# Attention probabilities turned by VectorE and DRAM instead of by TensorE

## The chip, the cores and the metric

The kernel runs on one core of one Trainium2 chip. Its engines each work through an instruction queue of their own and wait for one another by semaphores: TensorE (PE in the profile; PEld is its weight load), VectorE (DVE), ScalarE (ACT), GpSimd (POOL) and SyncE (SP), whose queue issues most of the DMAs. The metric is the device time of one execution in microseconds, as a median of several runs. Lower is better.

## The reference

The program is two layers of a diffusion backbone over 512 latent tokens and 256 context tokens of width 1024, in fp32. Layer 0 has differential attention (8 heads, each with two score maps of head size 64), layer 1 grouped-query attention (8 query heads and 2 key/value heads of size 128). Context queries read only context keys, and the last layer computes no context output.

```
h = rms_norm(x, pre_g) * (1 + scale) + shift          # same for the context with its own scale, shift
q, k, v, z = split(h @ w_in)                          # q, k get rotary positions on latent tokens
p  = softmax(q k^T * scale)                           # per head, 512 x 768 for latent queries
layer 0: o = softmax1 @ v - lam * softmax2 @ v;  o = rms_norm(o, subln_g) * (1 - lam_init)
layer 1: o = softmax @ v
y  = (o * silu(z)) @ w_out
x  = x + gate * rms_norm(y, post_g)
```

`scale`, `shift` and `gate` come from `silu(c) @ ada_w + ada_b` (adaLN).

## The kernel before

Every fp32 product is taken as three passes: an operand is split into a rounded high part (`hi`, written by ScalarE) and the rest (`lo`, a subtraction on VectorE or GpSimd), and TensorE adds hi*hi, hi*lo and lo*hi (`mm3`). Weights come in tiles of 128x1024 (`raw`, two buffers) through SP's DMA queue; ScalarE writes `whi`, GpSimd or VectorE writes `wlo`, into one of three slots from which TensorE reads them.

Tokens are in 6 tiles of 128: 4 latent ones and 2 of context. A head's queries are worked in halves of 256 tokens ("a pair" below: two units of 128 queries). In layer 0 each head has two latent pairs (`ch` 0 and 1) and one of context (`ch` 2); in layer 1 two. For a pair the steps are:

- `s_units` (layer 0) or `s1_units` (layer 1): scores of 128 queries against 768 keys into the PSUM tiles `sc`, VectorE takes the row maximum, ScalarE the exponential with its sum, VectorE the reciprocal, GpSimd multiplies the row by it (`scaled`). In layer 0 the second map is multiplied by -lambda and added to the first on VectorE (`SCALAR_TENSOR_TENSOR p<-p,sm,p`). The result is `p`, 128 queries by 768 keys.
- `tstep` in `pv_steps` and `pv1_steps`: the next product needs keys on partitions, so TensorE transposes `p` block by block, four 128x128 blocks (two key tiles of two units) into one PSUM bank, by `nc.tensor.transpose(...)` with the identity `ident`; in the profile these are `bk<-ident,p`. ScalarE then writes `ah` and VectorE `al`, the split of that bank. Three tsteps make up a pair.
- `mstep` (`pv_mm`): `v` times `ah` and `al`, six matmuls of 256 columns for each tstep, accumulated over the three.

The `v` projection (`v_mm` in layer 0, `proj_tok` in layer 1) is turned round against the others: the tokens `h` are the stationary operand, 128 of them to a weight load, and the weights stream 256 columns. The profile writes such a matmul as `bk<-whi,h` (moving operand first).

The order of each engine is written by a planner. `flow` lays steps out by due times, with the projections' matmuls filled in between (`piece`), and `Plan.schedule` then sorts all operations by the prices of `Plan.price`, taking on each engine the operation that can start first. The result is fixed at build time: each engine, and SP's queue, then works in that order and waits where it must. All operations are recorded by one helper, so they all carry its line (L395 before); the profile is read by tile names.

Of the kernel before, what the change touches and what calls it, by code (L numbers as in the profile page):

```python
# [8 lines left out]
F32 = mybir.dt.float32  # L9
# [6 lines left out]
P = 128  # L16
# [31 lines left out]
WBUFS = 3  # L48
XE = [2, 2, 2, 2, 3, 3]
# [24 lines left out]
AB = 3  # L74
MEM = 227168
AHEAD_OPS = 1500
MARGIN = 1.08
SLOT = {}
# [28 lines left out]
class Plan:  # L107


    def __init__(self, mem, psum, sizes):  # L110
        self.mem, self.sizes = mem, sizes
        self.psum = dict(psum)
        self.banks = {t.tensor.name: t.free_size() for t in psum.values()}
        self.width = mem.shape[1]
        self.ops, self.offs, self.tail, self.seen = [], [0], None, {}
        self.marks = []
        self.pools, self.stack = [], {"left": [], "right": []}
        for q in QUEUE:
            setattr(self, q, Queue(self.add, QUEUE[q]))


    def pool(self, name, side="left", psum=False):
        return Pool(self, name, side, psum)

# [41 lines left out]
    def add(self, q, meth, args, kw):  # L166
# [14 lines left out]
        for aps_, w in ((ins, 0), (outs, 1)):  # L181
            for ap in aps_:
                if ap.space == bass.MemoryType.DRAM:
                    continue
                name, spans, parts = self.places(ap)
                if name not in self.banks:
# [103 lines left out]
    def schedule(self, rank):  # L290
# [15 lines left out]
        while len(order) < count:  # L306
# [27 lines left out]
            elif op.kind == "D":  # L334
                s = max(s, land.pop(0))
                go = s + (330 if e == "SP" else 450)
                dma = max(dma, go + 300) + op.cost / 350.0
                end = max(go + 1700 + op.cost / 350.0, dma) + (800 if op.cost == 131072 else 300)
# [47 lines left out]
class Emit:  # L386
# [7 lines left out]
    def add(self, eng, meth, args, kw):  # L394
        self.ops.append(getattr(eng, meth)(*args, **kw))  # L395
        return self.ops[-1]

# [81 lines left out]
def tile_backbone(  # L479
# [30 lines left out]
    ps1 = ctx.enter_context(pl.pool("ps1", psum=True))  # L510

# [24 lines left out]

    def mm3(o, ahi, alo, bhi, blo, start, stop):
# [4 lines left out]
    def pv_mm(o, vh, vl, c, ah, al, kt, first, last):  # L542
        terms = [(v, a, e) for v, a in ((vh, ah), (vl, ah), (vh, al)) for e in range(2)]
        for i, (v, a, e) in enumerate(terms):
            nc.tensor.matmul(o, v[:, kt + e, c], a[:, e * 256:e * 256 + 256], start=first and i == 0, stop=last and i == 5)
# [492 lines left out]
    def v_mm(o, w, t, k_lo=0, k_hi=KT, first=True, last=True):  # L1038
        for kt in range(k_lo, k_hi):
            sl = slice(t * P, (t + 1) * P)  # L1040
# [82 lines left out]
    with pl.pool("t0") as t0:  # L1123
# [140 lines left out]
        def s_units(h, qts):  # L1264
            res = []

            def unit(qt):
# [11 lines left out]
                prev = None  # L1279
                for j in range(nk // w):  # L1280
                    c = slice(k0 + j * w, k0 + j * w + w)
                    for i, (a, b) in enumerate(((qh, kh_), (qh, kl_), (ql, kh_))):
                        for m in (1, 0):
                            r = slice(m * 64, m * 64 + 64)
                            with after(prev), chained(prev):
                                prev = nc.tensor.matmul(
                                    sc[m][:, j if nk == T else m, :w], a[r, tok], b[r, c], start=i == 0, stop=i == 2)
                for m in range(2):
# [3 lines left out]
                    pt = t0.tile([P, T], F32, tag=f"p{m}", name=nm("p"), bufs=6 if m == 0 else 2)[:, :nk]  # L1292
                    pv_ = pt.rearrange("p (j n) -> p j n", j=2) if nk == T else pt
                    nc.scalar.activation(pv_, scv, AF.Exp, bias=mx, accum_out=l[:, m:m + 1])
# [5 lines left out]
                    else:  # L1300
                        nc.vector.tensor_tensor(r, r, nlam, ALU.mult)
                        nc.vector.scalar_tensor_tensor(ps_[0], pt, r, ps_[0], ALU.mult, ALU.add)
                        res.append(ps_[0])

            def unit_ctx():
# [3 lines left out]
                for qt in (NQ, NQ + 1):  # L1309
                    tok = slice(qt * P, (qt + 1) * P)  # L1310
                    for i, (a, b) in enumerate(((qh, kh_), (qh, kl_), (ql, kh_))):
                        for m in (1, 0):
                            r = slice(m * 64, m * 64 + 64)
                            with after(prev), chained(prev):
                                prev = nc.tensor.matmul(
                                    sc[m][:, qt - NQ, :C], a[r, tok], b[r, S:T], start=i == 0, stop=i == 2)
                l = [small(2), small(2)]
                pts = []
                for m in range(2):
                    mx = small(2)  # L1320
                    nc.vector.tensor_reduce(mx, sc[m][:, :, :C], AX.X, ALU.max, negate=True)
                    pt = t0.tile([P, T], F32, tag=f"p{m}", name=nm("p"), bufs=6 if m == 0 else 2)
# [19 lines left out]
        def pv_steps(h, at, ch, after, ts, ms):  # L1342
            kts = range(6) if ch < 2 else range(4, 6)
            st = {}

            def tstep(kt):
# [9 lines left out]
                nc.scalar.copy(ah, tr)  # L1356
                nc.vector.tensor_tensor(al, tr, f32(ah), ALU.subtract)
                st[kt] = ah, al

            def mstep(kt):  # L1360
# [6 lines left out]
                pv_mm(o, vh, vl, vc, ah, al, kt, kt == kts[0], kt == kts[-2])  # L1367
                if kt == kts[-2]:
# [5 lines left out]
                    nc.scalar.copy(gT[h][:, sl], o)  # L1374
# [185 lines left out]
    def proj_tok(o, w, t):  # L1560
# [132 lines left out]
    with pl.pool("t1", "right") as t1p:  # L1693
# [45 lines left out]
        def k_tr(m, kr):  # L1739
# [4 lines left out]
            sl = slice(m * P, (m + 1) * P)  # L1744
            nc.scalar.copy(kh[:, :, sl], tv)
            nc.vector.tensor_tensor(kl[:, :, sl], tv, f32(kh[:, :, sl]), ALU.subtract)
# [15 lines left out]
        for what, m in KV:  # L1762
# [7 lines left out]
            else:  # L1770
# [3 lines left out]
                run(proj_tok(o, wk if what == "k" else wv, m))  # L1774
# [74 lines left out]
        def s1_units(h, ms):  # L1849
            res = []  # L1850

            def unit(m):
# [4 lines left out]
                for j in range(2):  # L1857
                    c = slice(j * 384, j * 384 + 384)
                    mm3(sc[:, j, :384], qa[:, sl], qb[:, sl], kh[:, g, c], kl[:, g, c], True, True)
# [6 lines left out]
                pt = t1q.tile([P, T], F32, tag="p", name=nm("p"), bufs=5)  # L1866
                l = small()
                nc.scalar.activation(pt.rearrange("p (j n) -> p j n", j=2), scv, AF.Exp, scale=sr, bias=nmx, accum_out=l)
                nc.vector.reciprocal(l, l)
                scaled(EN1, pt, pt, l)  # L1870
                res.append(pt)
# [3 lines left out]
        def pv1_steps(h, at, ch, after, ts, ms):  # L1875
            g = h // 4
            st = {}

            def tstep(kt):
                tr = trp()  # L1880
                for e in range(2):
                    for i, a in enumerate(at):
                        nc.tensor.transpose(tr[:, e * 256 + i * P:e * 256 + (i + 1) * P], a[:, (kt + e) * P:(kt + e + 1) * P], ident)
# [4 lines left out]
                nc.scalar.copy(ah, tr)  # L1888
                nc.vector.tensor_tensor(al, tr, f32(ah), ALU.subtract)
                st[kt] = ah, al  # L1890

            def mstep(kt):
# [5 lines left out]
                pv_mm(o, vh, vl, c, ah, al, kt, kt == 0, kt == 4)  # L1898
                if kt == 4:
                    if ch == 0:  # L1900
                        gT1[h] = t1p.tile([P, 512], F32, tag="g1", name=nm("g1"), bufs=8)
                    (nc.scalar.copy if EG1 == "a" else nc.vector.tensor_copy)(gT1[h][:, ch * 256:ch * 256 + 256], o)
# [217 lines left out]
```

## Time and profile before

| | |
|---|---|
| Median of 3 runs | 808.6 us (806.29 to 809.25) |
| Profiled execution | 808.79 us, span 807.0 us |
| Granted TensorE clock | 0.993 |
| Busy, share of the span | PE 97%, weight loads 87%, DVE 59%, ACT 60%, POOL 54% |
| Instructions | 14,385 |
| DMA | 77.78 MB, mean 96 GB/s |

A row of the groups reads: line, engine, operation, out<-in with buffer numbers left out, partitions x elements, count, then busy time in us and the mean ns of one, then the idle time of the engine ahead of these instructions and what ended it. The busy time of a group on PE counts overlapped time once, so the mean of one matmul (from its start to its modelled end) is longer than the distance between two of them; how far apart they start is read from the timeline.

### The profile page before, as it was taken

Reading aid. Unit: us, or ns where it says so; the run is one execution under the profiler, and the core shown is the slowest. Engines: PE = TensorE matmul, PEld = TensorE weight load, DVE = VectorE, ACT = ScalarE, POOL = GpSimd, SP = SyncE. Lnnn points to the kernel's source line nnn. Section 1 sums busy time; section 2 is a strip of 40 time slices with the busy share of each in tenths; the row PEclk is TensorE's granted clock in tenths of the full one; section 3 lists DMA queues with packets and bytes.
Section 4 is the critical chain, followed back from the end, with each engine's and each line's share of the span. In section 5 each row is a group of like instructions: output and inputs, shape, how many; then the busy total and the mean of one; then the engine's idle time right before and its main releaser. Section 6 shows DMA issues by size and latency. Waiting matters only on the chain.

```text
span 807.0 us, 14385 instructions
## 1 busy us (share of the span) xinstructions
PE 786.4 (97%) x5482; PEld 699.8 (87%) x5482; DVE 473.6 (59%) x824; ACT 482.0 (60%) x1083; POOL 437.4 (54%) x512
## 2 busy tenths in 40 slices
PE   7899999999999999999999999999999999999997
PEld 5779888889887898797989998898999899898886
DVE  3425787774847546656546743788346455655625
ACT  5524577684565645666538843784466676768622
POOL 4545776874585654757923312366887646644101
PEclk9899999999999999999999999999999999999999
DMA  9951120132142431323430152035321200201112
GB/s 302 363 180 67 65 75 31 40 108 89 40 158 79 144 105 53 105 80 96 165 106 27 62 227 79 1 89 175 120 70 53 96 11 27 79 27 55 51 53 105
DMA packets 41541, 77.78 MB, mean 96 GB/s; under 512 B 3584, under 2 KB 18688, under 8 KB 41472
## 3 DMA queue, kind: packets, MB, share of 16 engines
q1 hardware_dynamic: 38048, 71.71, 27.4%
q10 hardware_dynamic: 3424, 5.15, 1.8%
q8 instruction: 43, 0.70, 0.4%
q14 instruction: 26, 0.21, 0.1%
HBM read 70.56 MB, written 2.10 MB: 90 GB/s over the span
## 4 chain that ended last, share of the span: by engine, by line
PE 91%; DVE 3%; ACT 2%; DMA 2%; issue 1%; SPq 0%; POOL 0%; ACTq 0%; DVEq 0%; POOLq 0%
PE bk L395 75%; PE sc L395 16%; DMA ag<-in_ada_w 1%; DMA raw<-in_post_g 1%; DVE gacc L395 1%; DMA gw<-in_ada_w 0%; ACT whi L395 0%; SPq L395 0%; DVE h L395 0%; ACT sq L395 0%; DVE hf L395 0%; ACT p L395 0%; DVE sw L395 0%; DVE gate L395 0%; ACT jk L395 0%
## 5 line engine op out<-in xcount | busy, mean ns | idle before, releaser
L395 PE MATMUL bk<-whi,h 128*128 128x256 f32 (+1 forms) x1184 | 244.6, 299 | 2.0 <-DVE kn L395 1.3
L395 PE MATMUL bk<-h,whi 128*128 128x512 f32 (+2 forms) x832 | 225.6, 351 | 0.0
L395 POOL TENSOR_TENSOR wlo<-raw,whi 128x256 fp32r<-128x256 f32 x200 | 162.5, 839 | 76.7 <-ACT whi L395 75.3
L395 PEld LDWEIGHTS bk<-whi,h 128*128 128x128 f32 x1184 | 191.0, 189 | 14.6 <-issue 4.9
L395 PE MATMUL bk<-wlo,h 128*128 128x256 f32 (+1 forms) x592 | 176.5, 299 | 0.0
L395 PEld LDWEIGHTS bk<-h,whi 128*128 128x128 f32 x832 | 144.1, 188 | 16.5 <-issue 4.4
L395 PE MATMUL bk<-h,wlo 128*128 128x512 f32 (+2 forms) x416 | 145.7, 351 | 0.0
L395 DVE TENSOR_REDUCE sm<-sc 128x1 f32<-128x768 f32 (+2 forms) x114 | 101.0, 897 | 25.7 <-PE sc L395 25.4
L395 PEld LDWEIGHTS bk<-wlo,h 128*128 128x128 f32 x592 | 111.7, 189 | 4.8 <-issue 1.4
L395 POOL TENSOR_SCALAR p<-p,sm 128x768 f32<-128x768 f32 (+1 forms) x80 | 68.4, 858 | 77.6 <-DVE sm L395 72.8
L395 DVE TENSOR_TENSOR al<-bk,ah 128x512 fp32r<-128x512 f32 x104 | 69.4, 685 | 39.3 <-ACT ah L395 38.8
L395 ACT CAST whi<-raw 128x1024 fp32r<-128x1024 f32 (+1 forms) x70 | 71.7, 1026 | 31.9 <-PE bk L395 27.7
L395 ACT ACTIVATE p<-sc,sm 128x768 f32<-128x768 f32 (+1 forms) x96 | 72.9, 762 | 21.6 <-DVE sm L395 15.6
L395 ACT CAST ah<-bk 128x512 fp32r<-128x512 f32 x104 | 59.0, 590 | 43.5 <-PE bk L395 43.1
L395 PEld LDWEIGHTS bk<-h,wlo 128*128 128x128 f32 x416 | 78.4, 188 | 7.5 <-issue 1.3
L395 PE MATMUL bk<-ident,p 128*128 128x128 f32 x416 | 64.3, 275 | 1.6 <-DVE ql L395 1.1
L395 PEld LDWEIGHTS bk<-ident,p 128*128 128x128 f32 x416 | 49.0, 141 | 11.4 <-issue 2.0
L395 DVE SCALAR_TENSOR_TENSOR p<-p,sm,p 128x768 f32<-128x768 f32 (+1 forms) x48 | 53.4, 1120 | 3.3 <-POOL p L395 0.5
L395 ACT ACTIVATE jk<-bk 128x128 f32<-128x128 f32 (+4 forms) x66 | 22.7, 345 | 53.5 <-PE bk L395 34.4
L395 POOL TENSOR_TENSOR sz<-sz,za 128x384 f32<-128x384 f32 (+1 forms) x24 | 29.4, 1227 | 40.3 <-ACT za L395 39.7
L395 PE MATMUL sc<-qk,qk 64*128 64x384 f32 (+1 forms) x480 | 50.6, 341 | 0.0
L395 DVE RECIPROCAL sm<-sm 128x1 f32<-128x1 f32 (+1 forms) x114 | 18.1, 159 | 52.0 <-ACT p L395 51.5
(191 smaller groups left out, 1375.5 us busy)
## 6 DMA issues: line engine op xcount, KB each, us to landing
raw<-in_a_w SPq DMA_DIRECT2D x30, 512.0 KB, 3.5
araw<-in_ada_w SPq DMA_DIRECT2D x12, 1024.0 KB, 5.3
raw<-in_b_w SPq DMA_DIRECT2D x20, 512.0 KB, 3.5
ag<-in_ada_w SPq DMA_DIRECT2D x32, 256.0 KB, 6.5
raw<-in_w_out SPq DMA_DIRECT2D x16, 512.0 KB, 3.6
sw<-qr ACTq DMA_DIRECT2D x32, 128.0 KB, 2.1
gw<-in_ada_w SPq DMA_DIRECT2D x8, 512.0 KB, 4.1
xt<-in_x SPq DMA_DIRECT2D x4, 512.0 KB, 5.1
```

Of the source, the lines that this page charges most:

```text
L395: self.ops.append(getattr(eng, meth)(*args, **kw))
```

## The change

For latent pairs TensorE's transposes are left out. The two units of a pair write one tile `pp` (128 queries by 24 key blocks by 2 units by 32), and `turn` does the rest: VectorE transposes every 32x32 block of it in place (one instruction over 1536 elements, `STREAM_TRANSPOSE`), SP stores the whole tile to a DRAM scratch `dr` (768 KB) and loads it back in four DMAs (192 KB each), each to one group of 32 partitions of the tile `at`, which then has keys on its partitions. `ah` and `al` are split from `at` in SBUF, no longer from a PSUM bank. The context pairs of layer 0 still go through TensorE.

Key j of block order no longer sits where it sat: partition 32a+j of key tile k holds latent token 4(32a+j)+k, or context token 2(32a+j)+k. So the `v` projection takes its 128 tokens with a step (`keys`: every fourth latent token, every second context token), and `k` is written in another order (`ordered`, in layer 0 three ACT casts and three POOL subtractions a head where two and two stood; in layer 1 in `k_tr`). The outputs of `pv_mm` come out as (block, unit, 32) and are put back by the copy into `gT` (`heads_out`). Buffers: `p` had 6 (layer 0) and 5 (layer 1), `pp` and `at` have 2 each, `ah` and `al` 2 where they had 3, `dr` 6. The planner prices a DMA of 192 KB at 570 ns of its queue and others at 450, and lets every landing be 1 us later.

```diff
+DPAD = 1000
-AB = 3
+AB = 2
+P0B = 2
+ATB = 2
+PPB = 2
+DRSPLIT = 1
+DRB = 6
+PEWAY = ((), ())
...
+    def keys(src, t):
+        if t < NQ:
+            return src[:, :S].rearrange("p (x k) -> p k x", k=4)[:, t]
+        return src[:, S:].rearrange("p (x k) -> p k x", k=2)[:, t - NQ]
+
+    def ordered(t, r, lo, k):
+        a = by_a(t, 192)[:, :, :P] if k == 4 else by_a(t, 192)[:, :, P:]
+        return a.rearrange("p a (k j) -> p a k j", k=k), r.rearrange("p (a j k) -> p a k j", a=4, k=k)
...
+            if moved:
+                d, b = by_a(o, 64), a.rearrange("p (b e x) -> p e b x", b=4, e=2)[:, e]
+            else:
+                d, b = o, a[:, e * 256:e * 256 + 256]
+            nc.tensor.matmul(d, v[:, kt + e, c], b, start=first and i == 0, stop=last and i == 5)
+
+    def turn(pool, pp):
+        flat = pp.rearrange("p b u x -> p (b u x)")
+        nc.vector.transpose(flat, flat)
+        at = pool.tile([P, 4, 384], F32, tag="at", name=nm("at"), bufs=ATB)
+        for lo in range(0, 4, 4 // DRSPLIT):
+            n = 4 // DRSPLIT
+            dr = drp.tile([P // DRSPLIT, 4 * 384], F32, tag="dr", name=nm("dr"), bufs=DRB)
+            nc.sync.dma_start(dr[:, :], flat[32 * lo:32 * (lo + n), :])
+            for a in range(4):
+                nc.sync.dma_start(
+                    at[32 * a:32 * a + 32, lo:lo + n, :],
+                    dr.rearrange("(q j) (a c) -> a j q c", j=32, c=384)[a])
+        return at
...
+    def split_at(ah, al, src, moved):
+        hi, lo = (by_a(ah, P), by_a(al, P)) if moved else (ah, al)
+        nc.scalar.copy(hi, src)
+        nc.vector.tensor_tensor(lo, src, f32(hi), ALU.subtract)
...
-            mm3(o, hhi[kt][:, sl], hlo[kt][:, sl], wh[:, c], wl[:, c], first and kt == 0, last and kt == KT - 1)
+            mm3(o, keys(hhi[kt], t), keys(hlo[kt], t), wh[:, c], wl[:, c], first and kt == 0, last and kt == KT - 1)
...
-            for r, hi, lo in ((rr[0], *qk[h][:2]), (rr[1], *qk[h][2:])):
+            nc.scalar.copy(qk[h][0], rr[0])
+            eng.tensor_tensor(qk[h][1], rr[0], f32(qk[h][0]), ALU.subtract)
+            for lo_, hi_, k in ((0, S, 4), (S, T, 2)):
+                (hi, r), (lo, _) = (ordered(t, rr[1][:, lo_:hi_], lo_, k) for t in qk[h][2:])
                 nc.scalar.copy(hi, r)
                 eng.tensor_tensor(lo, r, f32(hi), ALU.subtract)
...
+                if nk == T and qt % 2 == 0:
+                    pair[qt // 2] = t0.tile([P, 24, 2, 32], F32, tag="pp", name=nm("pp"), bufs=PPB)
...
-                        res.append(ps_[0])
+                        if not moved:
+                            res.append(ps_[0])
+                        elif qt % 2:
+                            res.append(turn(t0, pair[qt // 2]))
...
             def tstep(kt):
-                tr = trp()
-                for e in range(2):
-                    j = kt + e - kts[0]
-                    for i, a in enumerate(at):
-                        nc.tensor.transpose(tr[:, e * 256 + i * P:e * 256 + (i + 1) * P], a[:, j * P:(j + 1) * P], ident)
+                if not moved:
+                    tr = trp()
...
-                nc.scalar.copy(ah, tr)
-                nc.vector.tensor_tensor(al, tr, f32(ah), ALU.subtract)
+                split_at(ah, al, at[0][:, :, kt * 64:kt * 64 + P] if moved else tr, moved)
...
-            mm3(o, h1hi[:, kt, sl], h1lo[:, kt, sl], wh[:, c], wl[:, c], kt == 0, kt == KT - 1)
+            a, b = (keys(t_[:, kt, :], t) if perm else t_[:, kt, sl] for t_ in (h1hi, h1lo))
+            mm3(o, a, b, wh[:, c], wl[:, c], kt == 0, kt == KT - 1)
```

TensorE in layer 1, around the `v` product of head 0's first pair (`ah`, `al`: the split probabilities; `vh`, `vl`: the values; `whi`, `wlo` with `h`: a query projection that fills in). Before, with the transposes of the next pair between:

```order
L395 MATMUL bk_69<-ah_6975,vh 128x256 x2
L395 MATMUL bk_69<-ah_6975,vl 128x256 x2
L395 MATMUL bk_69<-al_6976,vh 128x256
L395 MATMUL bk_70<-ident,p_6908 128x128
L395 MATMUL bk_69<-al_6976,vh 128x256
L395 MATMUL bk_69<-ah_7019,vh 128x256 x2
L395 MATMUL bk_69<-ah_7019,vl 128x256 x2
L395 MATMUL bk_69<-al_7020,vh 128x256 x2
```

and now:

```order
L411 MATMUL bk_70<-ah_6920,vh 128x256 x2
L411 MATMUL bk_70<-ah_6920,vl 128x256 x2
L411 MATMUL sc_74<-kl,qh_6635 128x384
L411 MATMUL sc_74<-kh,ql_6636 128x384
L411 MATMUL bk_71<-whi_6653,h_706_5239 128x256
L411 MATMUL bk_71<-whi_6653,h_705_5238 128x256
L411 MATMUL bk_70<-al_6921,vh 128x256 x2
L411 MATMUL bk_70<-ah_6967,vh 128x256 x2
```

The `ident,p` rows are gone; between the product's matmuls stand those of a later unit's scores and of the projection.

SP's queue in layer 1, where both pairs of head 0 and the first of head 1 go through DRAM (`raw`: weights and bias rows). Before:

```order
L395 DMA raw_6928<-in_b_w 128x1024
L395 DMA raw_6937<-in_b_w 128x1024
L395 DMA raw_7243<-in_b_w 128x1024
L395 DMA raw_7252<-in_b_w 128x1024
L395 DMA raw_7409<-in_ada_b 128x512
```

and now:

```order
L411 DMA dr_6793<-pp_6724 128x1536
L411 DMA at_6792<-dr_6793 32x4x384 x4
L411 DMA raw_7182<-in_b_w 128x1024
L411 DMA dr_6961<-pp_6857 128x1536
L411 DMA raw_7191<-in_b_w 128x1024
L411 DMA at_6960<-dr_6961 32x4x384 x4
L411 DMA dr_7076<-pp_7030 128x1536
L411 DMA at_7075<-dr_7076 32x4x384 x4
```

A store and its four loads stand among the weight loads, and the loads wait for the store in front of whatever follows them in the queue.

VectorE in the same place (`sm`: maxima and reciprocals; `ta`: rotary work of a query projection). Before, `al` is taken from a PSUM bank:

```order
L395 TENSOR_REDUCE sm_7006<-sc_72 128x1
L395 TENSOR_TENSOR ta_6988<-bk_68,ropeb 128x256
L395 TENSOR_TENSOR al_7020<-bk_69,ah_7019 128x512
L395 TENSOR_TENSOR al_7046<-bk_70,ah_7045 128x512
L395 TENSOR_TENSOR tb_6989<-bk_68,ropeb 128x2x64 x2
```

and now from `at`, with the block transposes of a later pair behind:

```order
L411 RECIPROCAL sm_7070<-sm_7070 128x1
L411 TENSOR_TENSOR al_6921<-at_6792,ah_6920 128x512
L411 TENSOR_TENSOR al_6968<-at_6792,ah_6967 128x512
L411 TENSOR_TENSOR al_7017<-at_6792,ah_7016 128x512
L411 STREAM_TRANSPOSE pp_7030<-pp_7030 128x1536
L411 TENSOR_REDUCE sm_7149<-sc_75 128x1
```

The three splits of a pair now stand together, since they all wait for the same four loads.

More of the change, by code (lines that the diff above doesn't have):

```diff
@@ L182, in add @@
             for ap in aps_:
-                if ap.space == bass.MemoryType.DRAM:
+                far = ap.space == bass.MemoryType.DRAM
+                if far and all(ap.tensor.name != d.tensor.name for d in self.drams):
                     continue
-                name, spans, parts = self.places(ap)
-                if name not in self.banks:
+                name, spans, parts = (ap.tensor.name, [(0, 2048)], 1) if far else self.places(ap)
+                if name not in self.banks and not far:
                     at = spans[0][0]
@@ L540, in mm3, with pv_mm, dma_way, unit_view @@
         nc.tensor.matmul(o, alo, bhi, start=False, stop=stop)
-    def pv_mm(o, vh, vl, c, ah, al, kt, first, last):
+    def pv_mm(o, vh, vl, c, ah, al, kt, first, last, moved=False):
         terms = [(v, a, e) for v, a in ((vh, ah), (vl, ah), (vh, al)) for e in range(2)]
         for i, (v, a, e) in enumerate(terms):
-            nc.tensor.matmul(o, v[:, kt + e, c], a[:, e * 256:e * 256 + 256], start=first and i == 0, stop=last and i == 5)
+            if moved:
[16 more added lines that the diff above has]
+        return at
+    def dma_way(layer, h, ch):
+        return (h, ch) not in PEWAY[layer]
+    def split_at(ah, al, src, moved):
+        hi, lo = (by_a(ah, P), by_a(al, P)) if moved else (ah, al)
+        nc.scalar.copy(hi, src)
+        nc.vector.tensor_tensor(lo, src, f32(hi), ALU.subtract)
+    def unit_view(pp, u):
+        return pp[:, :, u, :]
+    def unit_row(pp, u):
+        return pp.rearrange("p b u x -> p (b u x)")[:, u * T:u * T + T]
+    def heads_out(dst, o, moved):
+        if moved:
+            return dst.rearrange("p (u b i) -> p b u i", u=2, b=4), o.rearrange("p (b u i) -> p b u i", b=4, u=2)
+        return dst, o
     ident = con.tile([P, P], F32, name="ident")
@@ L1264, in s_units @@
         def s_units(h, qts):
-            res = []
+            res, pair = [], {}
             def unit(qt):
@@ L1344, in pv_steps @@
             st = {}
+            moved = ch < 2 and dma_way(0, h, ch)
             def tstep(kt):
-                tr = trp()
-                for e in range(2):
-                    j = kt + e - kts[0]
-                    for i, a in enumerate(at):
-                        nc.tensor.transpose(tr[:, e * 256 + i * P:e * 256 + (i + 1) * P], a[:, j * P:(j + 1) * P], ident)
+                if not moved:
+                    tr = trp()
+                    for e in range(2):
+                        for i, a in enumerate(at):
+                            src = a[:, (kt + e - kts[0]) * P:(kt + e - kts[0] + 1) * P]
+                            nc.tensor.transpose(tr[:, e * 256 + i * P:e * 256 + (i + 1) * P], src, ident)
                 if h == 0 and ch == 0 and kt == 0:
@@ L1743, in k_tr @@
             tv = tr[:, :256].rearrange("p (j n) -> p j n", j=2)
-            sl = slice(m * P, (m + 1) * P)
-            nc.scalar.copy(kh[:, :, sl], tv)
-            nc.vector.tensor_tensor(kl[:, :, sl], tv, f32(kh[:, :, sl]), ALU.subtract)
+            kd = [t.rearrange("p g (a n) -> p g a n", a=4) for t in (kh, kl)]
+            k = 4 if m < NQ else 2
+            for b in range(1 if m < NQ else 2):
+                a, c = (m, slice(0, P)) if m < NQ else (2 * (m - NQ) + b, slice(P, 192))
+                hi, lo = (t[:, :, a, c].rearrange("p g (k j) -> p g k j", k=k) for t in kd)
+                src = tv[:, :, b * 64:b * 64 + 32 * k].rearrange("p g (j k) -> p g k j", k=k)
+                nc.scalar.copy(hi, src)
+                nc.vector.tensor_tensor(lo, src, f32(hi), ALU.subtract)
         def k_rope(m, o, r):
@@ L1773, in tile_backbone @@
                 o = pj(256)
-                run(proj_tok(o, wk if what == "k" else wv, m))
+                run(proj_tok(o, wk if what == "k" else wv, m, what == "v"))
                 if late:
@@ L1877, in pv1_steps @@
             st = {}
+            moved = dma_way(1, h, ch)
             def tstep(kt):
[L1880 to L1883, printed above, removed]
+                if not moved:
+                    tr = trp()
+                    for e in range(2):
+                        for i, a in enumerate(at):
+                            src = a[:, (kt + e) * P:(kt + e + 1) * P]
+                            nc.tensor.transpose(tr[:, e * 256 + i * P:e * 256 + (i + 1) * P], src, ident)
                 if h == 0 and ch == 0 and kt == 0:
```

110 lines of the change are left out of this document (78 added, 32 removed).

## The prediction, made before the changed kernel had run

> **What bounds the kernel now.** First the page's busy shares, the slices and the chain that ended last:
>
> ```profile
> PE 786.4 (97%) x5482; PEld 699.8 (87%) x5482; DVE 473.6 (59%) x824; ACT 482.0 (60%) x1083; POOL 437.4 (54%) x512
> PE   7899999999999999999999999999999999999997
> PEclk9899999999999999999999999999999999999999
> PE 91%; DVE 3%; ACT 2%; DMA 2%; issue 1%; SPq 0%; POOL 0%; ACTq 0%; DVEq 0%; POOLq 0%
> ```
>
> TensorE is busy in nearly every slice at full clock and makes up 91% of the chain; no other engine is above 60%. Busy TensorE need not be dense, so I looked at three stretches (start, layer 0, layer 1) and, in the timeline, at the distances between starts:
>
> ```profile
> 0.00:60.00 60.00, 52.69 (x345) 39.67 (x346) 21.82 (x56) 27.94 (x51) 28.94 (x46) 0.91 0.87 283
> ...
> 300.00:400.00 100.00, 99.61 (x702) 86.57 (x702) 59.21 (x98) 62.20 (x130) 64.54 (x65) 1.00 0.31 97
> ...
> 600.00:700.00 100.00, 97.85 (x704) 92.74 (x703) 53.90 (x108) 66.64 (x161) 64.90 (x89) 1.00 0.16 48
> ```
>
> ```profile
> 301.58 0.28 PE L395 MATMUL bk<-wlo,h 128*128 128x256 f32 x1
> ...
> 301.94 0.28 PE L395 MATMUL bk<-wlo,h 128*128 128x256 f32 x1
> ...
> 302.30 0.60 PE L395 MATMUL bk<-ident,p 128*128 128x128 f32 x4
> 302.65 0.36 PE L395 MATMUL bk<-wlo,h 128*128 128x256 f32 x1
> 302.85 0.40 PE L395 MATMUL bk<-whi,h 128*128 128x256 f32 x2
> ```
>
> The windows' columns are PE, PEld, DVE, ACT, POOL busy us, clock, DMA share, GB/s. Only 0.4 us in 100 are idle on TensorE in layer 0 and 2.2 in layer 1. The timeline shows three 256-column matmuls every 0.36 us (0.118 each; 355 to 360 ns in neighbouring triples), with no gap. So TensorE's own work is the time: what is taken from it is saved, as long as nothing late takes its place.
>
> **The change, part by part.**
>
> *Transposes removed.* In the timeline four of them and one 256-column matmul take 302.85 - 302.30 = 0.55 us, so four cost 0.55 - 0.118 = 0.43. There are 32 latent pairs of three steps, 96 blocks: 96 x 0.43 = 41.3 us. The group's busy time gives the upper end:
>
> ```profile
> L395 PE MATMUL bk<-ident,p 128*128 128x128 f32 x416 | 64.3, 275 | 1.6 <-DVE ql L395 1.1 <-DVE al L395 0.4
> L395 PEld LDWEIGHTS bk<-whi,h 128*128 128x128 f32 x1184 | 191.0, 189 | 14.6 <-issue 4.9 <-DVE kn L395 1.6 <-DVE kl L395 0.8
> ```
>
> 384/416 of 64.3 is 59 us, but it counts latency that the next matmul overlaps. I take 41.3.
>
> *Stationary `h` with a step.* 720 matmuls of the v projections (30 token tiles x 8 x 3) now load every fourth latent token (480) or every second context token (240). No row of before loads weights with a step. Lower end: nothing, as in the row above, the same load dense. How much room there is follows from the transposes: 0.43/4 = 0.108 us apart though they stream only 128 columns, half of what takes 0.118; so a load of 128 columns takes 0.108 and hides behind 256 columns by 0.010 only. Upper end: each of the 720 takes twice that, 720 x (0.216 - 0.118) = 71 us; if loads only ceased to overlap (0.189, the row), 51. I take 0, since the dense load is the nearest row, and keep the upper end as a rival. Score and PV operands keep runs of 32 or 64 elements and write PSUM contiguously: 0.
>
> *VectorE, ScalarE, GpSimd.*
>
> ```profile
> L395 DVE TENSOR_TENSOR wlo<-raw,whi 128x1024 fp32r<-128x1024 f32 x18 | 23.5, 1304 | 15.9 <-ACT whi L395 15.9
> L395 DVE TENSOR_TENSOR al<-bk,ah 128x512 fp32r<-128x512 f32 x104 | 69.4, 685 | 39.3 <-ACT ah L395 38.8
> L395 ACT CAST h<-hf 128x512 fp32r<-128x512 f32 x12 | 7.3, 619 | 0.0
> L395 POOL TENSOR_TENSOR qk<-qr,qk 128x768 fp32r<-128x768 f32 x14 | 27.5, 1972 | 6.9 <-ACT qk L395 6.0 <-PE bk L395 0.8
> ```
>
> No row has a block transpose. From 512 to 1024 elements a subtraction grows by 0.62 us, so 1536 give 1.92; lower end half, if it ran at two elements a step, upper end 3.8 if at half rate. I take 1.92: 32 x 1.92 = 61 us, VectorE to 535 of 777, 69%: beside TensorE's work. The split from SBUF is a 512-element cast as in `h<-hf`, 0.62. The k split gains one cast and one subtraction a head, and its reads have a step; if GpSimd's 1.97 doubled, eight heads would be 2 us later each, behind the 20 us and more of fill that the new order has there. These cost nothing on the path while the fill lasts; without it 16 us in layer 0.
>
> *The way through DRAM.*
>
> ```profile
> araw<-in_ada_w SPq DMA_DIRECT2D x12, 1024.0 KB, 5.3
> out_x<-u SPq DMA_DIRECT2D x6, 256.0 KB, 2.1
> out_x<-u SPq DMA_DIRECT2D x2, 128.0 KB, 1.8
> raw<-in_ada_b SPq DMA_DIRECT2D x4, 256.0 KB, 3.6
> sw<-qr ACTq DMA_DIRECT2D x32, 128.0 KB, 2.1
> ag<-in_ada_w SPq DMA_DIRECT2D x32, 256.0 KB, 6.5
> 331.74 0.38 SPq L395 DMA_DIRECT2D araw<-in_ada_w  x1
> SPq L395 <- ACT whi L395: 194.5, 27, 20.9
> SPq L395 <- POOL wlo L395: 168.5, 41, 9.5
> SPq L395 <- DVE wlo L395: 112.0, 11, 31.0
> ```
>
> The store of 768 KB lies between 3.3 us (the two `out_x` rows: 0.3 more per 128 KB) and 5.3; I take 4.0. A load of 192 KB lies between 2.1 and 3.6, I take 2.9, and up to 6.5 where many are under way (`ag`, the start). Issues take 0.38 each. SP gets 160 issues, 61 us; it spends 475 us in these three waits for weight buffers, so its time is free, but its order is not: a weight load behind `at` waits for the store (4.0), and a store behind a weight load waits for a buffer (up to 31 us in the rows). Traffic grows by 32 x 2 x 0.786 = 50 MB on 78, or 165 GB/s on average, under the 283 GB/s that the first 60 us move.
>
> Does it reach `v` in time? The longest chain for its room is in layer 1:
>
> ```profile
> L395 DVE TENSOR_REDUCE sm<-sc 128x1 f32<-128x768 f32 x96 | 90.3, 949 | 24.9 <-PE sc L395 24.6
> L395 ACT ACTIVATE sm<-sm,qrs 128x1 f32<-128x1 f32 x32 | 9.6, 299 | 7.7 <-DVE sm L395 7.5
> L395 ACT ACTIVATE p<-sc,sm,qrs 128x768 f32<-128x768 f32 x32 | 31.8, 994 | 2.6 <-PE bk L395 1.4
> L395 DVE RECIPROCAL sm<-sm 128x1 f32<-128x1 f32 x100 | 15.9, 159 | 40.9 <-ACT p L395 40.4
> L395 POOL TENSOR_SCALAR p<-p,sm x32: 904/912/1407, 595.4 to 740.2; 128x768 f32<-128x768 f32 x32
> L395 ACT ACTIVATE p<-sc,sm,qrs x32: 973/994/1020, 593.1 to 738.8; 128x768 f32<-128x768 f32 x32
> ```
>
> 0.95 + 0.30 + 0.99 + 0.2 (the sum read out, an estimate from the exponential's row) + 0.16 + 0.91 = 3.5; block transposes 1.9; store 0.4 + 4.0; loads 3 x 0.38 + 2.9; casts 0.62 + 0.69: 15.2 us from the last score matmul to the first PV matmul. In the new order the least that lies between them in layer 1 (head 3, first pair) is 100 matmuls of 256 columns, 36 of 384 and 4 transposes: 100 x 0.118 + 36 x 0.17 (an estimate by columns) + 0.43 = 18.4 us; most pairs have 19 to 28, in layer 0 all 21 to 60. So the way is covered, with 3 us to spare where it is tightest. The two `pp` buffers: units come every (738.8 - 593.1)/31 = 4.7 us, a pair every 9.4, less 1.3 of transposes 8.1. A buffer is held from the first unit's exponential to the store's landing, 4.05 + 8.6 = 12.6, and two allow 16.2. Again 3.6 us to spare. If both margins break, the next units' scores stand in TensorE's queue and so does everything behind them.
>
> In layer 1 the old order had a similar margin and left 2.2 us in 100 idle; with three more engines' queues and two DMA landings in the chain I take 0.5 us more for each of 16 pairs and 2 for layer 0: +10, between 0 and 30.
>
> **Sum**, against the profiled execution's 808.8 us (span 807.0, 1.8 around it; the median 808.6 is 0.2 lower): 808.8 - 41.3 + 10 = 777.5. Forecast 777 us, 0.961 of before. Its own range is 767 (no new idle) to 792.
>
> **Rivals.**
>
> B, slower: weight loads with a step of four take twice as long, and the v projections become bound by them: 480 x (0.216 - 0.118) = +47 us, 824 us; all 720 would make it 848. It decides from the point where the 480 cost 31 us, that is 0.183 us a matmul, or a load 1.7 times the dense 0.108; at 1.5 times the sum is 799, still faster. For it speaks that loads hide by 0.010 us only; against it that no row has such a load.
> [...]
>
> C, the landings are late: with the store at 6.5 and a load at 6.5 the chain is 15.2 + 2.5 + 3.6 = 21.3 us, more than 18.4 to 21 for about half of layer 1's pairs; two pairs in flight share a wait, so some 16 x 1.2 = 20 us beyond the forecast: 797. `ag` at 6.5 speaks for it, though from the start where slices are full; 48 GB/s in layer 1 speaks against it.
>
> D, no gain: TensorE's freed 41 us are waited away for weights, since SP's queue now mixes weights with stores and GpSimd splits weights at 65% busy in both windows: 806 us. Against it: weights are split a slot ahead, and the idle time in the row of weight loads above names neither `wlo` nor `whi`.
>
> **How the numbers follow.** Forecast 0.47, B 0.33, C 0.14, D 0.06. Less than 0.5% (4 us) either way is what a measurement of this kernel cannot tell from no change. Faster: the forecast's 0.47, C's 0.12 and 0.02 of B and D, 0.61. Same: 0.05 (D, and B at a load of 1.7 times). Slower: 0.34. The range runs from 767 to 829: it holds the forecast's, C, D and most of B (815 to 829), and leaves out B with all 720 loads.
>
> **What would show it.** Right: no `ident,p` rows but 32 of the context pairs; `bk<-whi,h` with three starts in 0.36 us in the v projections too; PE busy near 745 us; `dr` landing near 4 us and `at` near 3 to 4. Wrong: v matmuls 0.2 us apart with longer weight loads (B); PV matmuls idle on DVE `al`, behind ACT `ah` and DMA `at`, in layer 1 by more than 15 us (C); idle on `wlo` or `whi` (D). A block transpose of 4 us or more would lengthen every chain by 2 and break the margins as in C.

## The result and the profile after

The changed kernel takes 843.6 us (median of 4 runs, 842.1 to 845.4), the kernel before 807.4 (805.8 to 809.3): a ratio of 1.045, 95% interval 1.041 to 1.049. It is slower, where the forecast said 777, and it lies above the whole range. The profiled execution took 844.7 us, with a span of 842.9.

The page of the changed kernel: busy shares, the chain that ended last by engine, the groups of the V projections' matmuls and weight loads, of the turned probabilities, and the DMA issues (KB each, median us from issue to landing).

```profile
PE 810.5 (96%) x5098; PEld 720.4 (85%) x5098; DVE 534.9 (63%) x859; ACT 485.4 (58%) x1093; POOL 456.9 (54%) x519
PE 61%; DMA 6%; DVE 6%; issue 4%; ACT 4%; POOL 3%; SPq 1%; ACTq 1%; DVEq 0%; POOLq 0%
...
L411 PE MATMUL bk<-whi,h 128*128 128x256 f32 (+1 forms) x1184 | 288.5, 331 | 3.5 <-DVE tb L411 1.6
L411 PEld LDWEIGHTS bk<-whi,h 128*128 128x128 f32 x1184 | 232.4, 227 | 17.6 <-issue 6.0
...
L411 PE MATMUL bk<-wlo,h 128*128 128x256 f32 (+1 forms) x592 | 195.1, 330 | 0.0
...
dr<-pp SPq DMA_DIRECT2D x32, 768.0 KB, 3.8
at<-dr SPq DMA_DIRECT2D x128, 192.0 KB, 4.6
```

```profile
L411 PE MATMUL bk<-ident,p 128*128 128x128 f32 x32 | 5.4, 296 | 1.3 <-DVE gate L411 1.3
...
L411 DVE TENSOR_TENSOR al<-at,ah 128x512 fp32r<-128x512 f32 x96 | 85.0, 905 | 28.1 <-ACT ah L411 24.6 <-PE bk L411 3.0
L411 DVE STREAM_TRANSPOSE pp<-pp 128x1536 f32<-128x1536 f32 x32 | 56.6, 1768 | 2.0 <-POOL pp L411 2.0
```

384 transposes are gone from TensorE, and yet it is busy for 24.1 us more (810.5 against 786.4). Its idle time grew by 11.8 us (842.9 - 810.5 = 32.4, against 20.6). Together that is the whole 35.9 us of span. So waiting is the smaller part of it: the work itself became longer, although the transposes are gone. The two groups that grew by much are those with the V projections' matmuls. In the kernel before they were:

```profile
L395 PE MATMUL bk<-whi,h 128*128 128x256 f32 (+1 forms) x1184 | 244.6, 299 | 2.0 <-DVE kn L395 1.3
...
L395 PE MATMUL bk<-wlo,h 128*128 128x256 f32 (+1 forms) x592 | 176.5, 299 | 0.0
```

Their busy time grew by 43.9 and 18.6 us, and no other TensorE group's by more than 1.5. A weight load of `bk<-whi,h` went from 189 to 227 ns on average over all 1184, most of which still read dense columns.

The timeline of the changed kernel shows it directly, first TensorE in a latent tile of a V projection (start, duration), then in a context tile:

```profile
192.98 0.63 PE L411 MATMUL bk<-whi,h 128*128 128x256 f32 x2
193.45 0.40 PE L411 MATMUL bk<-wlo,h 128*128 128x256 f32 x1
193.68 0.63 PE L411 MATMUL bk<-whi,h 128*128 128x256 f32 x2
194.15 0.40 PE L411 MATMUL bk<-wlo,h 128*128 128x256 f32 x1
...
211.92 0.28 PE L411 MATMUL bk<-wlo,h 128*128 128x256 f32 x1
212.04 0.40 PE L411 MATMUL bk<-whi,h 128*128 128x256 f32 x2
212.28 0.28 PE L411 MATMUL bk<-wlo,h 128*128 128x256 f32 x1
```

The groups of weight loads in the same two stretches:

```profile
L411 PEld LDWEIGHTS bk<-whi,h 128*128 128x128 f32 x8 | 2.3, 326 | 0.0
...
L411 PEld LDWEIGHTS bk<-whi,h 128*128 128x128 f32 x7 | 1.1, 196 | 0.2 <-issue 0.2
```

In the latent tile (every fourth token) three matmuls take 194.15 - 193.45 = 0.70 us, 0.234 each; in the context tile (every second token) 212.28 - 211.92 = 0.36, 0.120 each, about as in the kernel before (0.118). The same matmul of 256 columns waits for its weights where they have a step of four: 326 ns a load instead of 189. With a step of two a load takes 196, which still hides. 480 x (0.234 - 0.118) = 56 us.

### The profile page after: what moved, and what is told of

It reads as the page before. It is cut to its first block, busy times and chain, and to the rows that moved or that the text cites. A ratio compares the mean times of both kernels' runs of the same rounds, so it can differ in the third digit from the quotient of the medians.

```text
span 842.9 us, 14017 instructions
## 1 busy us (share of the span) xinstructions
PE 810.5 (96%) x5098; PEld 720.4 (85%) x5098; DVE 534.9 (63%) x859; ACT 485.4 (58%) x1093; POOL 456.9 (54%) x519
## 4 chain that ended last, share of the span: by engine, by line
PE 61%; DMA 6%; DVE 6%; issue 4%; ACT 4%; POOL 3%; SPq 1%; ACTq 1%; DVEq 0%; POOLq 0%
PE bk L411 52%; PE sc L411 9%; DMA at<-dr 4%; DVE al L411 2%; DMA dr<-pp 2%; DVE pp L411 1%; ACT ah L411 1%; POOL wlo L411 1%; SPq L411 1%; DVE sm L411 1%; DMA sw<-qr 1%; ACT whi L411 1%; ACTq L411 1%; POOL qr L411 1%; ACT p L411 0%
## 5 line engine op out<-in xcount | busy, mean ns | idle before, releaser
L411 PE MATMUL bk<-whi,h 128*128 128x256 f32 (+1 forms) x1184 | 288.5, 331 | 3.5 <-DVE tb L411 1.6
L411 PEld LDWEIGHTS bk<-whi,h 128*128 128x128 f32 x1184 | 232.4, 227 | 17.6 <-issue 6.0
L411 PEld LDWEIGHTS bk<-wlo,h 128*128 128x128 f32 x592 | 134.8, 228 | 4.8 <-issue 1.6
L411 POOL TENSOR_SCALAR pp<-pp,sm 128x768 f32<-128x768 f32 x64 | 64.9, 1013 | 89.3 <-DVE sm L411 77.4
L411 DVE TENSOR_TENSOR al<-at,ah 128x512 fp32r<-128x512 f32 x96 | 85.0, 905 | 28.1 <-ACT ah L411 24.6
L411 ACT CAST ah<-at 128x512 fp32r<-128x512 f32 x96 | 57.5, 618 | 26.0 <-PE bk L411 17.6
L411 DVE STREAM_TRANSPOSE pp<-pp 128x1536 f32<-128x1536 f32 x32 | 56.6, 1768 | 2.0 <-POOL pp L411 2.0
L411 ACT ACTIVATE p<-sc,sm 128x768 f32<-128x768 f32 (+1 forms) x64 | 43.9, 689 | 9.1 <-DVE sm L411 4.3
L411 PEld LDWEIGHTS sc<-qk,qk 64*128 64x128 f32 x480 | 39.6, 191 | 9.4 <-issue 3.5
L411 DVE RECIPROCAL sm<-sm 128x1 f32<-128x1 f32 (+1 forms) x114 | 16.9, 151 | 44.4 <-ACT p L411 32.6
L411 ACT ACTIVATE za<-za 128x384 f32<-128x384 f32 (+1 forms) x72 | 39.8, 559 | 5.5 <-DVE za L411 4.0
```

## The experiments

**Dense weight loads, everything else as changed.** Two ways of undoing the step. In the first, blocks of 32 tokens take the place of every fourth token; K and V use the same new order.

```diff
     def keys(src, t):
-        if t < NQ:
-            return src[:, :S].rearrange("p (x k) -> p k x", k=4)[:, t]
-        return src[:, S:].rearrange("p (x k) -> p k x", k=2)[:, t - NQ]
+        return src[:, t * P:(t + 1) * P]
...
-        return a.rearrange("p a (k j) -> p a k j", k=k), r.rearrange("p (a j k) -> p a k j", a=4, k=k)
+        return a.rearrange("p a (k j) -> p a k j", k=k), r.rearrange("p (k a j) -> p a k j", a=4, k=k)
```

Layer 1's `k_tr` writes the same order, four runs of 32 a tile.

> The changed kernel with the tokens of a tile in blocks of 32 (token = 128 k + 32 a + j), so that every weight load of the V projections reads 128 neighbouring columns; K's split reads contiguous runs too. All else, the turn on VectorE and the way through DRAM among it, stays. Theory L (the loads with a step of four hold TensorE up): 480 matmuls go from 0.234 to 0.118 us, 843.6 - 56 = 788 us, between 778 and 796, so faster than before. Theory R (the way through DRAM, VectorE's longer work and the contention from both cost the time, and a shorter V projection only turns into waiting for `al`): 835 to 845 us, with TensorE idle on `al`, behind `ah` and `at`, by 40 us more.

In the second only `keys` is dense.

> The changed kernel with only the V projections' weight loads dense; K keeps its order and its reads with a step, so values meet other keys than in the reference (that part of the computation differs). Theory L: 788 us, as in the run with blocks; what lies between the two is K's reads with a step on GpSimd and ScalarE (0 to 5 us). Theory R: 835 to 845 us.

Measured: 794.9 us with blocks (0.984 of before, 0.981 to 0.987) and 790.2 with dense V loads alone (0.979, 0.976 to 0.982). Both are as theory L said; theory R is out, since the way through DRAM is unchanged in both. From the changed kernel to the second, 843.6 - 790.2 = 53.4 us went with the indexing in `keys` alone. (The granted clocks of the two profiled executions differ, 0.985 and 0.996. Against blocks, also at 0.985, it is 843.6 - 794.9 = 48.7 us, with 37.3 - 32.4 = 4.9 us more of idle time.) Its page, the row of the loads:

```profile
L411 PEld LDWEIGHTS bk<-whi,h 128*128 128x128 f32 x1184 | 190.5, 188 | 19.0 <-issue 5.7 <-DVE tb L411 1.9 <-ACT g L411 1.2
```

The kernel with blocks computes what the reference does and beats both kernels. K's reads with a step, which the second kept, show no cost: the second is even the faster one, for which see the clock below.

**The step alone, in the kernel before.** TensorE still turns the probabilities; only the tokens of the V projections take the step (in `v_mm` and `proj_tok`), with `keys` of the changed kernel, or with a step of two everywhere.

```diff
-            mm3(o, hhi[kt][:, sl], hlo[kt][:, sl], wh[:, c], wl[:, c], first and kt == 0, last and kt == KT - 1)
+            mm3(o, keys(hhi[kt], t), keys(hlo[kt], t), wh[:, c], wl[:, c], first and kt == 0, last and kt == KT - 1)
```

> The kernel before with only the tokens of the V projections taken with a step of four (latent) and two (context); no DRAM way, no block transposes, TensorE turns the probabilities as before. Values meet other keys than in the reference. Theory L: 807.4 + 56 = 863 us, and the V projections' triples 0.70 us apart in the latent tiles, 0.36 us in the context tiles. Theory R: 807 to 812 us.

> The kernel before with the tokens of all V projections taken with a step of two, latent ones too; values meet other keys than in the reference. [...] If any step slows a load and the context tiles hid it by other things: 830 to 863 us.

```diff
     def keys(src, t):
+        n = t // 2 * 256
+        return src[:, n:n + 256].rearrange("p (x k) -> p k x", k=2)[:, t % 2]
```

Measured: 860.8 us with steps of four and two (1.066, 1.063 to 1.068), 808.5 with a step of two in all tiles (1.002, 1.000 to 1.003). 860.8 - 807.6 = 53.2 us against the 56 worked out; the step of two is bounded by 3 us. (With the 0.120 us of the context tiles the 480 make 807.4 + 480 x 0.002 = 808.4; the 830 and more of a price on any step did not come.) In the timeline of the run with a step of four the triples are 0.70 us apart, and in the run with two 0.36:

```profile
193.52 0.40 PE L395 MATMUL bk<-wlo,h 128*128 128x256 f32 x1
193.75 0.63 PE L395 MATMUL bk<-whi,h 128*128 128x256 f32 x2
194.22 0.40 PE L395 MATMUL bk<-wlo,h 128*128 128x256 f32 x1
```

```profile
185.05 0.28 PE L395 MATMUL bk<-wlo,h 128*128 128x256 f32 x1
185.17 0.40 PE L395 MATMUL bk<-whi,h 128*128 128x256 f32 x2
185.41 0.28 PE L395 MATMUL bk<-wlo,h 128*128 128x256 f32 x1
```

So the loss is caused by the step, with no part of the DRAM way in it; and it is the size of the step that counts, not that there is one. That is shown for weight loads of 128x128 fp32 and these two steps: 196 ns at a step of two, in the changed kernel and in this run with two everywhere, and 326 at a step of four. At which step between them the price sets in, and what makes it, no run shows.

**Where the rest of the gain is.** With dense loads the sum of the prediction would give 777; the run with blocks took 794.9. Its page, waits and windows (PE, PEld, DVE, ACT, POOL busy us; clock; DMA share; GB/s):

```profile
PE 756.3 (95%) x5098; PEld 665.9 (84%) x5098; DVE 539.1 (68%) x857; ACT 483.7 (61%) x1091; POOL 456.9 (58%) x519
...
200.00:300.00 100.00, 95.84 (x623) 80.09 (x622) 71.07 (x100) 60.36 (x129) 68.08 (x64) 0.97 0.55 169
600.00:700.00 100.00, 91.02 (x570) 82.83 (x569) 77.27 (x117) 69.21 (x159) 72.58 (x87) 0.97 0.72 208
...
PE bk L411 <- DVE al L411: 4.0, 5, 2.4
PE bk L411 <- DVE gate L411: 3.4, 2, 2.1
PE bk L411 <- ACT ah L411: 2.9, 3, 1.6
PE bk L411 <- ACT sqs L411: 2.9, 3, 1.5
PE sc L411 <- DVE sm L411: 2.4, 1, 2.4
```

TensorE's idle time is 793.6 - 756.3 = 37.3 us, 16.7 over before; the forecast had 10. No releaser holds much of it: short waits for VectorE and ScalarE, at many places. Three kinds of runs asked which of them matters.

First, late landings: the loads read the DRAM tile that was stored two turns earlier, so they need not wait for their own store.

```diff
             nc.sync.dma_start(dr[:, :], flat[32 * lo:32 * (lo + n), :])
+            turned.append(dr)
+            dr = turned[max(0, len(turned) - 3)]
```

> The run with blocks, in which the four loads of a pair read the DRAM tile that the pair two turns earlier stored, so they need not wait for their own store (probabilities of another pair are used: that part of the computation differs; every instruction and byte stays). The chain loses the store's landing of 3.9 us. If late landings are what TensorE waits for in the run with blocks (rival C): 14.8 us of ScalarE's waits on `at` fall to under 5, and the time to 780 to 788 us. If VectorE's longer work, the hold of the `pp` buffers and contention with GpSimd are what it waits for: 792 to 797.

Measured: 792.3 us (0.981, 0.979 to 0.984), at the edge of no change. ScalarE's waits on `at` fell from 14.8 to 6.4 us, but TensorE stayed idle for 792.8 - 755.1 = 37.7 us, as before this edit: the largest of its waits is now another (`sc` on ACT `pp`, 4.1 us). The median is 2.6 us lower than with blocks, and the intervals overlap. Late landings are not what holds most of the time.

Second, VectorE: its subtraction `al<-at,ah` now has two operands in SBUF. In the run with blocks single ones last 0.64 to 2.28 us (0.68 from PSUM). Look at two of them beside GpSimd:

```profile
254.95 1.72 POOL L411 TENSOR_TENSOR qr<-qr,rope 128x512 f32<-128x512 f32 x1
255.44 1.77 DVE L411 TENSOR_TENSOR al<-at,ah 128x512 fp32r<-128x512 f32 x1
256.75 1.61 POOL L411 TENSOR_TENSOR qr<-qr,sw 128x512 f32<-128x512 f32 x1
257.14 0.15 DVE L411 RECIPROCAL sm<-sm 128x1 f32<-128x1 f32 x1
257.22 1.70 DVE L411 TENSOR_TENSOR al<-at,ah 128x512 fp32r<-128x512 f32 x1
```

The second one ends at 258.92, 0.56 us after GpSimd's instruction (258.36). In this trace 42 of the 96 last 0.75 us or more, and 40 of them end 0.53 to 0.56 us after the GpSimd instruction that was under way when they began; of the 104 that read PSUM in the kernel before, none lasts 0.70. They appear to stand until GpSimd is through. TensorE waited for the longest:

```profile
161.33 2.51 POOL L411 TENSOR_TENSOR gT<-gT,sz 128x768 f32<-128x768 f32 x1
162.11 2.28 DVE L411 TENSOR_TENSOR al<-at,ah 128x512 fp32r<-128x512 f32 x1
```

It ends at 164.39, and the matmul that reads it starts at 164.44, after a pause of 2.38 us (shown below). So the subtraction was moved to GpSimd itself, in both layers and then in layer 0 alone:

```diff
-        nc.vector.tensor_tensor(lo, src, f32(hi), ALU.subtract)
+        (nc.gpsimd if pool else nc.vector).tensor_tensor(lo, src, f32(hi), ALU.subtract)
```

> The run with blocks, with the 96 subtractions al<-at,ah on GpSimd instead of VectorE. There they lasted 0.64 to 2.28 us, the long ones 0.55 us more than what was left of a GpSimd instruction under way when they began. If this waiting (and VectorE's queue behind it) is what makes TensorE wait: VectorE goes from 539 to 451 us, GpSimd from 457 to some 580 (a subtraction there at 1.3 us by qk's 1.97 for 768 columns), and the time falls to 785 to 792 us. If it is the landing of `at`, no change: 793 to 797. If GpSimd's order is the tighter one (weights split late): 800 or more, with TensorE idle on wlo or al from GpSimd.

> The run with blocks, with the subtractions al<-at,ah on GpSimd in layer 0 alone and on VectorE in layer 1. With all of them on GpSimd, layer 1's first exponential came at 582.1 us (586.0 with none), but layer 1 then took 227 us instead of 207.6. If the two layers stand by themselves: 582.1 + 207.6 + 1.3 = 791 us, between 788 and 793. If what GpSimd gains in layer 0 is lost again behind it (weights for layer 1 late): 794 to 798.

Measured: 811.6 us (1.006, 1.004 to 1.009) with both layers, 792.7 (0.982, 0.980 to 0.984) with layer 0 alone. GpSimd's order is the tighter one; the longest of TensorE's waits, with both layers, became:

```profile
PE bk L411 <- POOL q L411: 8.0, 2, 4.7
```

With layer 0 alone the time came to the edge of the expected band, but its interval overlaps that of the run with blocks, and TensorE's idle time is the same (789.5 - 752.7 = 36.8 us). The waiting on GpSimd is seen in the trace, and TensorE behind it at one place; what it costs the kernel as a whole is not shown.

Third, one layer at a time, and half of layer 1, by the list of pairs that TensorE turns:

```diff
-PEWAY = ((), ())
+PEWAY = ((), tuple((h, c) for h in range(8) for c in range(2)))
```

> The run with blocks (dense weight loads), with the way through DRAM for layer 0's 16 pairs alone; layer 1's probabilities are turned by TensorE again. That run gained 12.7 us on the kernel before where the sum gave 30; its first exponential of layer 1 began at 586.0 us against 593.1, so 7 us were gained by then. If the loss lies in waits of each layer by itself: 807.6 - 7 = 800 us, between 797 and 803. If it is one layer alone that loses: 787 (layer 0 is sound and layer 1 loses) or 805 and more.

> The run with blocks, with the way through DRAM for layer 1's 16 pairs alone. If each layer has its own waits: 807.6 - 6 = 801 us, between 798 and 805. If layer 1's short cover (scores to PV) is what loses, layer 0 none: 805 or more, with TensorE idle on `ah` and `al` and a granted clock of 0.50 after the longest of these pauses.

> The run before this one (subtractions on GpSimd in layer 0), with only the first of each head's two pairs in layer 1 on the way through DRAM; the second is turned by TensorE. Layer 1 took 213.9 us with no pair on that way and 207.6 with 16. If it waits because pairs follow one another too closely for two buffers and for VectorE: eight pairs wait little and give most of 8 x 1.29 = 10 us: 785 to 789. If each pair waits by itself: half of 6.3 us, 793 to 796.

Measured: layer 0 alone 800.0 us (0.991, 0.990 to 0.993), as expected; layer 1 alone 815.2 (1.010, 1.008 to 1.012), which falls in the second branch (805 or more) but not for the reason given there, and half of layer 1 (with layer 0's subtractions on GpSimd) 801.8 (0.993, 0.991 to 0.995), outside both branches. Layer 1 alone was lost before layer 1 began: its first exponential came at 603.6 us, against 593.1 before, and from there to the end it took 209.7 us against 213.9. A pair that goes back to TensorE does not go back to the old kernel: the memory went to `pp` and `at`, so it has two buffers for `ah` and `al` instead of three and two pairs instead of five or six single tiles for `p`, and its scores are reordered on the way into PSUM. Which of these costs the 10 us was not separated, and so these runs say nothing clean about one layer's share; only that a mixture is worse than the whole.

**The clock.** Spans and mean granted clock of the kernel before, the changed one, blocks and dense V loads:

```profile
core 0: 807.0 us, clock 0.993
```

```profile
core 0: 842.9 us, clock 0.985
```

```profile
core 0: 793.6 us, clock 0.985
```

```profile
core 0: 787.3 us, clock 0.996
```

Blocks and dense V loads wait alike (37.3 and 36.5 us idle), and differ in the clock. The same pause stands in both (of blocks, then of dense V loads, the pause's row and the window around it):

```profile
164.44 0.51 PE L411 MATMUL bk<-al,vhi 128*128 128x256 f32 x2 [2.38 <-DVE al L411]
...
160.00:170.00 10.00, 7.54 (x47) 6.44 (x46) 9.69 (x11) 5.63 (x13) 8.39 (x8) 0.83 0.33 104
```

```profile
164.51 0.50 PE L411 MATMUL bk<-al,vhi 128*128 128x256 f32 x2 [2.38 <-DVE al L411]
...
160.00:170.00 10.00, 7.53 (x57) 6.71 (x56) 9.86 (x11) 7.05 (x17) 8.47 (x8) 1.00 0.29 95
```

With equal pauses one ran at full clock and recorded 57 matmuls in the window, the other at 0.83 and recorded 47. Read microsecond by microsecond, the clock with blocks was about half from 166.3 to 169.8, 3.4 us. That looks like a price of a pause that comes behind it, and by these two windows it depends on more than the pause's length (2.38 us in both). The traces show one regularity. With blocks the low stretches begin at 166.35, 261.92, 534.99 and 664.69 us: 95.57, 273.07 and 129.70 us apart, which is 28, 80 and 38 steps of 3.413 us. In the changed kernel the clock was 0.50 in six stretches ahead of the last matmul, which begin at 9.45, 64.07, 176.71, 282.52, 579.48 and 678.47 us: 16, 33, 31, 87 and 29 such steps apart; five last one step (9.45 to 12.87) and one two (282.52 to 289.35). Counted back in such steps from 166.35, the last step holds most of the pause. Dense V loads have a low stretch at 262.34, and counted back from it, the same pause is split over two steps (a row with blocks, then two with dense V loads):

```profile
162.94:166.35 3.41, 1.82 (x13) 1.62 (x14) 3.41 (x5) 1.87 (x5) 3.41 (x4) 1.00 0.36 133
...
159.94:163.35 3.41, 2.19 (x17) 1.96 (x15) 3.41 (x3) 2.41 (x6) 3.41 (x3) 1.00 0.46 148
163.35:166.77 3.42, 2.17 (x15) 1.88 (x15) 3.42 (x5) 2.22 (x5) 3.42 (x4) 1.00 0.26 102
```

TensorE was idle for 1.59 us of the one step, which came before the fall, and busy for the rest of its 3.41; of the other two it was idle for 1.22 and 1.25, and no fall came. Whether it is the place of a pause among these steps that decides, no run tested. How much idle time it takes is not shown: in the changed kernel the step ahead of a low stretch held from 0.00 to 1.87 us of it.

(1 - 0.985) x 793.6 = 11.9 us at a lost clock, against (1 - 0.993) x 807.0 = 5.6 before, makes 6.3 us that no term of the sum held. This is an upper estimate, since TensorE also idles at a low clock (1.18 us of the 6.83 from 282.52 on in the changed kernel): between blocks and dense V loads 11.9 - 3.1 = 8.8 us of lost clock go with 756.3 - 750.8 = 5.5 us of busy time.

## Why the prediction was wrong

- **The step that failed: "Stationary `h` with a step ... I take 0, since the dense load is the nearest row".** The term was 56 us by the timeline and 53 by two pairs of runs. The same paragraph had worked out that a load hides behind 256 columns by 0.010 us only, and rival B that the sign turns at 0.183 us a matmul, 1.7 times the dense 0.108; it was 0.234, 2.2 times. Nearness of a row was the wrong reason there: a row that lacks the very property in question (a step) says nothing on its price, and the margin of 0.010 us was the better evidence.
- **Rival B came true,** with its place and its 480 loads: a load with a step of four took 326 ns instead of 189 and set the pace of the stage; the 240 of the context tiles stayed hidden (0.120 us a matmul). Its price was 47, from 0.216 us a matmul; that such a load takes twice the dense 0.108, and that a step of two takes no more, no run of before shows, both were the author's assumptions. Measured were 0.234, hence 56, and 0.120. Its 824 us was too low by these 9 us, and by terms that it shared with the forecast: a full clock (up to 7 us) and the price of the transposes, below.
- **Transposes:** the group fell to 32, as said, but 41.3 us seems too much. The kernel before and the run with dense V loads have the same number of matmuls but for these 384, and TensorE's busy time fell by 786.4 - 750.8 = 35.6 us between them, at a clock 0.003 higher. In the run with dense V loads 808.8 - 41.3 + 15.9 (new idle: 787.3 - 750.8 - 20.6) - 2.5 (clock) = 780.9, and the profiled execution took 789.1. With four transposes at 0.35 us, the distance to the next start in the rows quoted (302.65 - 302.30), instead of 0.43 the saving is 33.6 and the sum 788.6. The prediction had also counted the longer start of the matmul behind them; the lower price fits better, but no run measured it alone. TensorE's busy time was to be near 745 us, and was 810.5 with the step and 750.8 without.
- **New idle time, +10 (0 to 30):** 11.8 in the changed kernel, 15.9 and 16.7 with dense loads, where TensorE's own work is shorter. Inside the bounds.
- **VectorE:** 535 us of busy time forecast, 534.9 measured, which was luck. A block transpose takes 1.77 us (1.92 forecast), 4.8 us less for 32. But `al` was priced as from PSUM: 905 ns on average, not 685, 21 us more for 96. The other 16 us came off many other groups, of which no term spoke (`p<-p,sm,p` and `pp<-p,sm,pp` together fell from 53.4 to 48.6 us, the reciprocals from 18.1 to 16.9).
- **The way through DRAM:** the store lands in 3.8 us (4.0), the loads in 4.6 (2.9, with 6.5 as the upper end). 1.7 us longer in a chain with 3 us to spare; rival C did not decide anything: in the run with early loads the median is only 2.6 us lower, within the noise. Rival D did not happen: no wait on weights is among the longest of TensorE's in the changed kernel.
- **What no step held:** the lower clock, at most 12.6 us at a lost clock (0.015 x 842.9) against 5.6. 808.8 - 41.3 + 56 + 11.8 + 7.0 = 842.3, where the execution took 844.7; with the lower price of the transposes it is 850, and with 53 for the loads 847.

## What to carry to other kernels

Ask of every stationary operand how its columns lie in SBUF: here fp32 values with a step of four made a load take 1.7 times as long (326 ns, 189 dense), and a load that hid behind 256 columns by a hair became the pace of the stage (0.234 us a matmul instead of 0.118). Where an order of tokens is free to choose, blocks of neighbours serve a 32x32 transpose as well as every fourth token (1.77 us for 1536 elements in both orders), and the same change is then 1.6% faster instead of 4.5% slower. When a prediction finds a margin of hundredths of a microsecond under an unknown cost, the unknown should carry the forecast, not a row that only resembles it.

## What the runs showed of the hardware that was not expected

- A weight load of 128x128 fp32: 188 ns dense, 196 with a step of two, 326 with a step of four; matmuls of 256 columns then start 0.118, 0.120 and 0.234 us apart.
- A 32x32 block transpose of 128x1536 fp32 on VectorE takes 1.77 us, 1.15 ns an element in each partition, hardly varying (1.76 to 1.78).
- A VectorE subtraction of 512 columns with both inputs in SBUF takes 0.64 to 2.28 us, and 0.67 to 0.69 with one input in PSUM. The long ones end 0.53 to 0.56 us after the GpSimd instruction that was under way when they began (40 of 42 with blocks).
- Equal pauses of 2.38 us on TensorE were followed by 3.4 us at half the clock in one kernel (0.83 over 160 to 170 us) and by none in another (1.00). The low stretches of the changed kernel last 3.41 or 6.83 us, at a clock of 0.50.
